# One bank for a whole output product, and a third accumulator for columns in place of a third for preparation

## The chip, the cores and the metric

The kernel runs on one core of one Trainium2 chip. The metric is the device time of one execution in microseconds (us), the median of several runs. A difference of less than about 1% can hardly be told from no change here.

## What is computed

One layer of an encoder is applied to two batches of 512 tokens by 1024 channels, with the same weights. Half of the mixed channels come from a bidirectional recurrence (RWKV-7), half from a two-dimensional neighbourhood attention:

```python
h = rms_norm(x, norm1_g)
proj = h @ w_in                                  # 1024 -> 3456 columns
rw_out = rwkv7_time_mix(shifted(proj[:, :1920])) # 512 channels, a scan in both directions
na_out = neighbourhood_attention(proj[:, 1920:]) # 512 channels, softmax over 8 x 16 neighbours
x = x + concatenate([rw_out, na_out], -1) @ w_out          # the output product
x = x + conv_ffn(x)                              # norm, w_up (1024 -> 5632), conv, gate, w_down
```

## The kernel before

Activations lie with channels on the 128 partitions and the 512 tokens along the row, so a weight column block is one PSUM bank of 128x512. Each such product is made of three matmuls per channel tile (high by high, low by high, high by low), to keep float32 accuracy.

`trunk` doesn't issue instructions. It records them, with a priority and with the tile that each reads and writes, and `Recorder.run` then makes one fixed order for each engine: at each step it takes, for the engine that comes free first, the ready instruction of the lowest priority number, by its own costs and latencies. A tile can only be placed once one of the buffers of its tag is free. `PBUFS` gives the number of PSUM banks of each tag: "mm" for columns of big products, "g" for the preparation of the recurrence and for the scores of the attention, and one bank each for "ch" (the chain of the scan), "y" and "x". They add up to eight. On the chip each engine works through its order as it stands.

The work goes in three stages.

- **Recurrence.** Eight groups (four channel tiles of batch 0, then of batch 1). `rwkv_prep`, `rwkv_products` (tiles `pg_G`) and `rwkv_turn` (`pg_V`, `pg_T`) prepare a group through the "g" banks; `rwkv_inverse` (`px_v`, `px_w`, `px_x`, and the short vector steps `tm`, `i_nr`) inverts 16 small triangles; `rwkv_chain` steps through eight chunks (`pch`, `py_y`). `proj` fills the rest of TensorE with columns of `w_in` (`pmm_in`), as work of low priority. The normalised input of one batch lies in 16 `H` tiles. They hold batch 0, then batch 1, and then batch 0 again (`norm1(0, False)`, tiles `po_x0nFalse`) for the columns that only the attention needs.
- **Attention.** Eight units, the four of batch 1 first (`ORDER = (1, 0)`). A unit's scores are `pg_sca`, its transposes `py_pta`, its sums `pch_oa` or `px_oa`, and its result goes through `py_ota` and `iW_ao` to the DRAM tile `mixd`.
- **Output product and feed-forward.** Columns of `w_out` in two halves: `w_out1` takes the four recurrence channel tiles of a batch, adds the input `x` and stores to the DRAM tiles `x1d` (product tiles `pmm_wp`); `w_out2` loads `x1d` again, multiplies the four attention channel tiles (`H_mb` or `AR_mb`, high and low) and adds. `norm2`, the `uf`, `up` and `dn` products follow.

```python
    w_out1(one)
    w_out1(two)
    w_out2(one)
    norm2(one)
```

Here `one` is batch 1 and `two` batch 0. `split_mix` loads four channel tiles of `mixd` through SyncE's queue, casts them (ScalarE) and makes the low parts (VectorE).

Of the kernel before, what the change touches and what calls it, by code (L numbers as in the profile page):

```python
# [20 lines left out]
P = 128  # L21
NB = 2
T = 512
# [8 lines left out]
STARTS = (0, 8, 24, 32)  # L32
GVB = 2
GAB = 1
PBUFS = {"mm": 2, "g": 3, "ch": 1, "y": 1, "x": 1}
BUFS = {
    "H": 16, "wr": 2, "wh": 3, "wl": 3, "po": 3, "gu": 4, "lora12": 2, "lora13": 2, "lora14": 2, 
    "AR": 2, "GV": GVB, "GA": GAB, "GR": 2, "UV": 2, "TT": 2, "bv": 2, "lw": 1, "ta": 1, "qd": 2, "rs": 2, "WC": 2, "Z": 2, "sw": 2,
# [6 lines left out]
ORDER = (1, 0)  # L45
# [14 lines left out]
MIXT = ("AR AR", "H " * 8)  # L60
# [6 lines left out]
X2T = (("UV", "UV"), ("GA", "BK"))  # L67
# [617 lines left out]
def trunk(ctx: ExitStack, tc: tile.TileContext, xT, win, wup, wout, wdn, lora_up, prm, cst, bias, out):  # L685
    nc = tc.nc
# [47 lines left out]
    def dram(name):  # L734
        return VTile([P, T], F32, real=dp.tile([P, T], F32, name=name))

    pd = [[dram(f"pd_{m}_{b}") for b in range(NB)] for m in range(NIN)]
    x1d = [[dram(f"x1d_{m}_{b}") for b in range(NB)] for m in range(8)]
    x2d = [[dram(f"x2d_{m}_{b}") for b in range(NB)] for m in range(8)]
    hd = [dram(f"hd_{m}") for m in range(8)]  # L740
    p1d = [dram(f"p1d_{m}") for m in range(NPRE)]
# [3 lines left out]
    nc = rec = Recorder(tc.nc, tc)  # L745
# [6 lines left out]
    def sb(tag, shape, name, dtype=F32):  # L752
        return sbp.tile(shape, dtype, tag=tag, name=f"{tag}_{name}", bufs=BUFS.get(tag, 1))

    def ps(tag, shape, name):
        return psp.tile(shape, F32, tag=tag, name=f"p{tag}_{name}", bufs=PBUFS[tag])

    first_w = list(FIRSTW)

    def load_w(src, n, name):  # L760
        pr = rec.prio
        rec.prio = first_w.pop(0) if first_w else min(pr, WPR)
        raw = sb("wr", [P, 4, P], name)
        nc.sync.dma_start(raw[:, :n], src)
        hi = sb("wh", [P, 4, P], name, F32R)
        nc.scalar.copy(hi[:, :n], raw[:, :n])
        lo = sb("wl", [P, 4, P], name, F32R)
        nc.gpsimd.tensor_tensor(lo[:, :n], raw[:, :n], hi[:, :n].bitcast(F32), ALU.subtract)
        rec.prio = pr
        return hi, lo  # L770

    def mm3(p, w, a, n, first, last):
        for k in range(n):
            ah, al = a(k)
            nc.tensor.matmul(p, w[0][:, k], ah, start=first and k == 0, stop=False)
            nc.tensor.matmul(p, w[0][:, k], al, start=False, stop=False)
            nc.tensor.matmul(p, w[1][:, k], ah, start=False, stop=last and k == n - 1)
# [53 lines left out]
    def wide(tags, name, dtype=F32):  # L831

        v = []
        for i, t in enumerate(tags.split()):
            n = 1 if t[0] == "H" or t[:4] == "lora" else 4
            x = sb(t, [P, n, T], f"{name}{i}", dtype)
            v += [x[:, j] for j in range(n)]
        return v
# [604 lines left out]
    rec.prio = 2 * FILL  # L1443
    banks = [t for t in PBUFS for _ in range(PBUFS[t])]
    nbank = [0]

    def bank(name):
        nbank[0] += 1
        return ps(banks[nbank[0] % 8], [P, T], name)

    x2, h2 = {}, {}

    one, two = ORDER

    def split_mix(b, k0, tags, name):

        v = wide(tags, f"{name}{b}", F32R)
        hi, lo = v[:4], v[4:8]
        for k in range(4):
            f = sb(("r", "k", "v", "i2")[k], [P, T], f"mx{b}{k0 + k}")  # L1460
            nc.sync.dma_start(f, mixd[k0 + k][b])
            nc.scalar.copy(hi[k], f)
            nc.vector.tensor_tensor(lo[k], f, hi[k].bitcast(F32), ALU.subtract)
        return hi, lo

    def gemm4(p, src, a, name):
        w = load_w(src, 4, name)
        mm3(p, w, lambda k: (a[0][k], a[1][k]), 4, True, True)

    def w_out1(b):  # L1470

        a = split_mix(b, 0, "GR GR", "ma")
        for n in range(8):
            p = ps("mm", [P, T], f"wp{n}{b}")
            gemm4(p, wout[n, :, :4], a, f"outa{n}{b}")
            x = sb(X1T[n % len(X1T)], [P, T], f"x1{b}{n}")
            nc.sync.dma_start(x, xT[b, :, n])
            nc.vector.tensor_add(x, x, p)
            nc.sync.dma_start(x1d[n][b], x)

    def w_out2(b):

        i = ORDER.index(b)
        a = split_mix(b, 4, MIXT[i], "mb")
        x2[b] = [sb(X2T[i][j], [P, 4, T], f"x2{b}{j}") for j in range(2)]
        for n in range(8):
            nc.sync.dma_start(x2[b][n // 4][:, n % 4], x1d[n][b])
        for n in range(8):
            p = ps("mm" if b == ORDER[0] else WOB[n % len(WOB)], [P, T], f"wo{n}{b}")
            gemm4(p, wout[n, :, 4:], a, f"outb{n}{b}")  # L1490
            xk = x2[b][n // 4][:, n % 4]
            nc.vector.tensor_add(xk, xk, p)
            nc.sync.dma_start(x2d[n][b], xk)

    def norm2(b):

        rs = sb("rs", [P, 4], f"f{b}")
        src = lambda k: x2[b][k // 4][:, k % 4]
        rms_scale(rms_sum(src, f"f{b}", lambda o, p, q: nc.vector.tensor_tensor(o, p, q, ALU.add), NTG[b == two]), rs, f"f{b}", NPS[b == two])
        if b == two:  # L1500
            v = wide(ACTB[1], f"g{b}", F32R)
            h2[b] = [None] * 4 + v[:4], [None] * 4 + v[4:]
        else:
            h2[b] = act_tiles(ACTB[0], f"g{b}")
        rms_split(src, row_scale(rs, f"f{b}", NPS[b == two]), lambda k: pv("n2g", k), *h2[b], f"f{b}", NPS[b == two], lambda k: nc.gpsimd.tensor_tensor if k % 4 in NPL else nc.vector.tensor_tensor, True)
        for k in range(8 if b == one else 0):
            nc.sync.dma_start(hd[k], src(k))
# [150 lines left out]
    G = {}  # L1658
    rec.prio = 1.5 * FILL
    mmb = lambda name: ps("mm", [P, T], name)  # L1660
    w_out1(one)
    w_out1(two)
    w_out2(one)
    norm2(one)
    halves_of("B11", one, 0)
    halves_of("B21", one, 1)
    w_out2(two)
    norm2(two)
    halves_of("B22", two, 1)
# [6 lines left out]
    for g, gn in enumerate(sizes):  # L1676
        for j in range(gn):
            up_pair(f0 + j, G, j)
        for n in range(8):
            w = load_w(wdn[n, :, f0 : f0 + gn], gn, f"dn{g}{n}")  # L1680
            for b in range(NB):
                p = bank(f"dn{g}{n}{b}")
# [3 lines left out]
                xk = sb(xl[nxl[0] % len(xl)], [P, T], f"xl{g}{n}{b}")  # L1686
# [64 lines left out]
```

## Time and profile before

| | |
|---|---|
| median of 3 runs | 1580.87 us (1577.47 to 1588.33) |
| the profiled execution | 1589.59 us, of which 1587.8 us are the span |
| TensorE (PE) busy | 1531.5 us, 96% of the span |
| VectorE (DVE) busy | 1195.3 us, 75% |
| ScalarE (ACT) busy | 800.1 us, 50% |
| GpSimd (POOL) busy | 286.4 us, 18% |
| HBM read, written | 152.05 MB, 57.67 MB |

The profiled execution is one execution; its time lies 0.55% above the median. PE is the engine that is nearly always busy. Matmuls overlap, so a busy PE is not PE at its best; how many matmuls start in a stretch, and how long it is idle, tells more.

### The profile page before, as it was taken

The numbers are of one execution on the slowest core, as the hardware profiler recorded it, in microseconds if no ns is written. First come the engines' busy times: TensorE is split into PE (matmuls) and PEld (weight loads), VectorE is DVE, ScalarE is ACT, GpSimd is POOL, SyncE is SP. The second block draws the span as 40 slices with busy tenths as digits, with TensorE's granted clock in tenths as the row PEclk, the third lists the DMA queues.
The fourth block names the chain that finished last, engine by engine and source line by source line (L and its number), as shares of the span: only waits on it lengthen the run. The fifth ranks groups of instructions, "written<-read, shape, count | busy, mean of one in ns | idle before, by whom it ended". The sixth has DMA issues, their size and how long they took to land.

```text
span 1587.8 us, 34480 instructions
## 1 busy us (share of the span) xinstructions
PE 1531.5 (96%) x13700; PEld 1210.2 (76%) x13700; DVE 1195.3 (75%) x2232; ACT 800.1 (50%) x1488; POOL 286.4 (18%) x284
## 2 busy tenths in 40 slices
PE   7997999999999999999998999999999999999998
PEld 5775777776777776788887877788788888888886
DVE  6878679877788675664685888959779578579666
ACT  5554565755655645577784454515335135234232
POOL 5223144321522312212230250000000000000000
PEclk8988999999999998999999999999999999999999
DMA  5522111222211225355777873383552631631535
GB/s 162 181 68 87 61 57 62 77 63 70 90 42 57 82 64 172 103 193 177 226 250 265 274 233 114 101 264 106 186 185 60 205 100 56 198 111 54 183 95 205
DMA packets 120401, 211.98 MB, mean 134 GB/s; under 512 B 13360, under 2 KB 22832, under 8 KB 120240
## 3 DMA queue, kind: packets, MB, share of 16 engines
q1 hardware_dynamic: 120096, 209.64, 40.6%
q8 instruction: 108, 1.77, 0.5%
q14 instruction: 53, 0.43, 0.1%
q10 hardware_dynamic: 144, 0.13, 0.0%
HBM read 152.05 MB, written 57.67 MB: 132 GB/s over the span
## 4 chain that ended last, share of the span: by engine, by line
PE 72%; DVE 7%; ACT 3%; DMA 2%; issue 2%; POOL 1%; SPq 0%; DVEq 0%; ACTq 0%; POOLq 0%
PE pmm_in L681 10%; PE pg_dn L681 6%; PE pmm_dn L681 4%; PE pch L681 2%; PE pmm_wp L681 2%; PE py_dn L681 2%; PE pch_dn L681 2%; PE px_dn L681 2%; PE pg_G L681 2%; PE py_y L681 1%; PE pmm_wo L681 1%; PE pg_T L681 1%; PE pg_sca L681 1%; PE px_x L681 1%; PE pg_wo L681 1%
## 5 line engine op out<-in xcount | busy, mean ns | idle before, releaser
L681 PE MATMUL pmm_in<-H_h,wh_in 128*128 128x512 f32 x848 | 311.3, 431 | 17.3 <-ACT H_h L681 6.2
L681 PEld LDWEIGHTS pmm_in<-H_h,wh_in 128*128 128x128 f32 x848 | 164.3, 199 | 57.8 <-issue 9.4
L681 PE MATMUL pmm_in<-H_h,wl_in 128*128 128x512 f32 x424 | 181.9, 429 | 5.2 <-DVE wl_in L681 2.8
L681 PEld LDWEIGHTS pmm_in<-H_h,wl_in 128*128 128x128 f32 x424 | 84.4, 199 | 23.2 <-DVE wl_in L681 4.0
L681 ACT CAST wh_in<-wr_in 128x512 fp32r<-128x512 f32 x108 | 66.4, 616 | 67.5 <-PE pmm_in L681 48.9
L681 DVE TENSOR_TENSOR wl_in<-wr_in,wh_in 128x512 fp32r<-128x512 f32 x82 | 62.5, 763 | 42.0 <-ACT wh_in L681 37.2
L681 ACT CAST wh_dn<-wr_dn 128x512 fp32r<-128x512 f32 (+1 forms) x48 | 27.8, 585 | 108.2 <-DMA wr_dn<-wdn_d 26.9
L681 PE MATMUL pg_G<-AR,BK 64*64 64x128 f32 x1024 | 69.2, 285 | 4.7 <-POOL BK L681 2.0
L681 POOL TENSOR_TENSOR wl_dn<-wr_dn,wh_dn 128x256 fp32r<-128x256 f32 x1 | 0.7, 738 | 374.3 <-ACT wh_dn L681 374.3
L681 PEld LDWEIGHTS pg_G<-AR,BK 64*64 64x64 f32 x1024 | 54.2, 137 | 16.7 <-issue 4.7
L681 POOL TENSOR_TENSOR sw<-S,WC 128x128 f32<-128x128 f32 x48 | 23.6, 492 | 180.1 <-DVE S L681 175.8
L681 ACT COPY UV<-pch 64x128 f32<-64x128 f32 x64 | 16.5, 258 | 68.8 <-DVE UV L681 42.9
L681 POOL TENSOR_TENSOR wl_in<-wr_in,wh_in 128x512 fp32r<-128x512 f32 x26 | 36.5, 1404 | 57.9 <-ACT wh_in L681 48.1
L681 DVE SCALAR_TENSOR_TENSOR po<-pmm_in,prm_s,po 128x511 f32<-128x511 f32 x58 | 43.2, 745 | 4.3 <-ACT po L681 3.6
L681 PE MATMUL pmm_wp<-GR_ma,wh_outa 128*128 128x512 f32 x128 | 44.2, 413 | 1.9 <-DVE Y_x L681 1.9
L681 ACT COPY i_na<-GA 32x512 f32<-32x512 f32 x32 | 35.0, 1094 | 19.5 <-DVE GA L681 19.1
L681 DVE SCALAR_TENSOR_TENSOR TT_ring<-pg_sca,rs_a,TT_ring 128x256 f32<-128x256 f32 x64 | 30.0, 478 | 16.7 <-PE pg_sca L681 9.4
L681 PE MATMUL pg_T<-cst_s,BK 64*64 64x64 f32 x1024 | 42.3, 221 | 0.0
L681 PEld LDWEIGHTS pg_T<-cst_s,BK 64*64 64x64 f32 x1024 | 36.7, 134 | 2.2 <-issue 1.2
L681 ACT ACTIVATE po_th<-ta_u 128x512 f32<-128x512 f32 x44 | 27.8, 632 | 19.6 <-DVE ta_u L681 13.4
L681 ACT ACTIVATE TT_ring<-TT_ring,mx_a 128x256 f32<-128x256 f32 x64 | 32.4, 507 | 5.1 <-DVE mx_a L681 4.6
L681 DVE TENSOR_TENSOR tm<-i_nr 128x15 f32<-128x15 f32 (+7 forms) x120 | 32.2, 269 | 2.5
(1903 smaller groups left out, 4568.6 us busy)
## 6 DMA issues: line engine op xcount, KB each, us to landing
wr_in<-win_d SPq DMA_DIRECT2D x108, 256.0 KB, 2.7
pd<-po SPq DMA_DIRECT2D x48, 256.0 KB, 2.1
GV_xl<-x2d SPq DMA_DIRECT2D x44, 256.0 KB, 4.0
wr_dn<-wdn_d SPq DMA_DIRECT2D x40, 256.0 KB, 2.7
x2d<-GV_xl SPq DMA_DIRECT2D x40, 256.0 KB, 3.1
i_up<-wup_d SPq DMA_DIRECT2D x33, 256.0 KB, 2.6
TT_ring<-bias_d SPq DMA_DIRECT2D x64, 128.0 KB, 2.7
up_xl<-x2d SPq DMA_DIRECT2D x22, 256.0 KB, 3.4
```

Of the source, the lines that this page charges most:

```text
L681: i.out = getattr(getattr(self.nc, i.eng), i.fn)(*[res(a) for a in i.args], **{n: res(a) for n, a in i.kw.items()})
```

## The change

`PBUFS` gives "mm" three banks and "g" two. For batch `one`, the two halves of the output product become one: a new `w_out` accumulates all eight channel tiles in one "mm" bank, loads `x` straight into the tile that `norm2` reads, and adds once. Batch `two` keeps its two halves.

```diff
-PBUFS = {"mm": 2, "g": 3, "ch": 1, "y": 1, "x": 1}
+PBUFS = {"mm": 3, "g": 2, "ch": 1, "y": 1, "x": 1}
...
-    x1d = [[dram(f"x1d_{m}_{b}") for b in range(NB)] for m in range(8)]
+    x1d = [dram(f"x1d_{m}") for m in range(8)]
...
+    def w_out(b):
+
+        a = split_mix(b, 0, "GR GR", "ma")
+        c = split_mix(b, 4, MIXT[ORDER.index(b)], "mb")
+        x2[b] = [sb(X2T[ORDER.index(b)][j], [P, 4, T], f"x2{b}{j}") for j in range(2)]
+        for n in range(8):
+            p = ps("mm", [P, T], f"wo{n}{b}")
+            w = load_w(wout[n, :, :4], 4, f"outa{n}{b}")
+            mm3(p, w, lambda k: (a[0][k], a[1][k]), 4, True, False)
+            w = load_w(wout[n, :, 4:], 4, f"outb{n}{b}")
+            mm3(p, w, lambda k: (c[0][k], c[1][k]), 4, False, True)
+            xk = x2[b][n // 4][:, n % 4]
+            nc.sync.dma_start(xk, xT[b, :, n])
             nc.vector.tensor_add(xk, xk, p)
             nc.sync.dma_start(x2d[n][b], xk)
...
-    w_out1(one)
     w_out1(two)
-    w_out2(one)
+    w_out(one)
     norm2(one)
```

Since the order is made anew, it differs nearly everywhere. Three places matter below.

The first is TensorE at the end of the attention. `py_ota30` is the last unit's last step; `mb02`, `mb03` are the high and `mb06`, `mb07` the low parts of the last two attention channel tiles of batch 0; `wp` and `wo` are the two halves of the output product, with column and batch behind them. Before:

```order
L681 MATMUL px_oa30_11006<-H_a305_10784,S_ring2_9172 128x64 x2
L681 MATMUL py_ota30_11131<-cst_s_62,H_a300_10074 128x128 x4
L681 MATMUL pmm_wp60_11137<-GR_ma00_10634,wh_outa60_11001 128x512
L681 MATMUL pmm_wp60_11137<-GR_ma01_10643,wh_outa60_11001 128x512
L681 MATMUL pmm_wp60_11137<-GR_ma00_10634,wl_outa60_11011 128x512
```

Now:

```order
L681 MATMUL px_oa30_11248<-H_a305_11054,S_ring2_9279 128x64 x2
L681 MATMUL py_ota30_11396<-cst_s_62,H_a300_9797 128x128 x4
L681 MATMUL pg_wo00_11315<-H_mb02_11412,wh_outb00_11100 128x512
L681 MATMUL pch_wo10_11257<-H_mb02_11412,wh_outb10_11153 128x512
L681 MATMUL pg_wo00_11315<-H_mb06_11414,wh_outb00_11100 128x512
L681 MATMUL pg_wo00_11315<-H_mb02_11412,wl_outb00_11114 128x512
L681 MATMUL pch_wo10_11257<-H_mb06_11414,wh_outb10_11153 128x512
L681 MATMUL pch_wo10_11257<-H_mb02_11412,wl_outb10_11161 128x512
L681 MATMUL pg_wo20_11351<-H_mb02_11412,wh_outb20_11223 128x512
L681 MATMUL pg_wo20_11351<-H_mb06_11414,wh_outb20_11223 128x512
L681 MATMUL pg_wo20_11351<-H_mb02_11412,wl_outb20_11239 128x512
L681 MATMUL pg_wo00_11315<-H_mb03_11433,wh_outb00_11100 128x512
```

Before, 24 matmuls of `wp` and then 96 of `wo` of batch 1 stood between the last unit and the first product that reads its batch's attention tiles; now all of those come earlier, and nine matmuls on `mb02` stand between `py_ota30` and the first that reads `mb03`.

The second place is VectorE where the `H` tiles take batch 0 again. Before:

```order
L681 SCALAR_TENSOR_TENSOR po_x0nFalse_8496<-po_x0nFalse_8496,prm_s,pmm_bca0False 128x512
L681 COPY UV_7953<-pch_8579 64x128
L681 TENSOR_TENSOR H_h_8592<-po_x0nFalse_8496,H_h_8576 128x512
L681 TENSOR_TENSOR S_8609<-pch_8579,WC_7275 128x128
L681 SCALAR_TENSOR_TENSOR po_x0nFalse_8541<-po_x0nFalse_8541,prm_s,pmm_bca0False 128x512
L681 TENSOR_TENSOR GV_8554<-GV_8554,pch_8579 128x128
L681 TENSOR_TENSOR H_h_8633<-po_x0nFalse_8541,H_h_8625 128x512
```

Now:

```order
L681 COPY UV_6962<-pch_7660 64x128
L681 TENSOR_TENSOR i_nr_7597<-i_nr_7597,tm_8064 128x11x5
L681 SCALAR_TENSOR_TENSOR po_x0nFalse_8138<-po_x0nFalse_8138,prm_s,pmm_bca0False 128x512
L681 TENSOR_TENSOR H_h_8234<-po_x0nFalse_8133,H_h_8214 128x512
L681 TENSOR_TENSOR tm_8064<-i_nr_7597 128x48
L681 TENSOR_TENSOR i_nr_7597<-i_nr_7597,tm_8064 128x12x4
L681 TENSOR_TENSOR H_h_8257<-po_x0nFalse_8138,H_h_8239 128x512
L681 TENSOR_TENSOR tm_8064<-i_nr_7597 128x39
L681 TENSOR_TENSOR wl_in_00_8269<-wr_in_00_7930,wh_in_00_8146 128x512
```

Before, the refill shared VectorE with the last chain (`UV`, `S`, `GV`), after the last inverse was done; now the refill comes one step of the recurrence earlier, among the steps of the last inverse (`tm`, `i_nr`).

The third place is TensorE in the preparation of group 3 (`pg_G3...`, beside the chain `pch_20` of group 2). Before:

```order
L681 MATMUL pg_G30011_3847<-AR_30_3438,BK_30_3447 64x128 x8
L681 MATMUL pg_G30100_3857<-AR_30_3438,BK_30_3447 64x128 x2
L681 MATMUL pg_G30101_3860<-AR_30_3438,BK_30_3447 64x128 x2
L681 MATMUL pg_G30100_3857<-AR_30_3438,BK_30_3447 64x128 x2
L681 MATMUL pg_G30101_3860<-AR_30_3438,BK_30_3447 64x128 x2
```

Now:

```order
L681 MATMUL pg_G30011_3886<-AR_30_3561,BK_30_3609 64x128 x8
L681 MATMUL pmm_in15_1_3788<-H_h112_1541,wh_in15_11_3767 128x512
L681 MATMUL pch_20_3743<-GV_200_3712,TT_20_2368 64x64 x4
L681 MATMUL pmm_in15_1_3788<-H_h14_1434,wl_in15_11_3818 128x512
L681 MATMUL pmm_in15_1_3788<-H_h15_1440,wh_in15_11_3767 128x512
L681 MATMUL pmm_in15_1_3788<-H_h113_1531,wh_in15_11_3767 128x512
L681 MATMUL pmm_in15_1_3788<-H_h15_1440,wl_in15_11_3818 128x512
L681 MATMUL pg_b30_3918<-ta_rk30_3908,bdr_65 128x512
L681 MATMUL pch_20_3743<-UV_20_3063,BT_20_3233 64x64 x4
L681 MATMUL pg_G30100_3929<-AR_30_3561,BK_30_3609 64x128 x8
```

Before, three product tiles followed each other in the three "g" banks; now a second tile of the pair is followed by columns and chain steps until a bank is read out.

## Rows read from the trace of the kernel before

**Rows 1.** The page: busy time, share of the span and instructions of each engine.

```profile
PE 1531.5 (96%) x13700; PEld 1210.2 (76%) x13700; DVE 1195.3 (75%) x2232; ACT 800.1 (50%) x1488; POOL 286.4 (18%) x284
```

**Rows 2.** Stretch, length; busy PE, PEld, DVE, ACT, POOL; granted clock, DMA share, GB/s.

```profile
150.00:600.00 450.00, 433.45 (x7946) 335.55 (x7934) 352.47 (x830) 263.85 (x490) 133.23 (x145) 0.99 0.22 69
600.00:650.00 50.00, 46.23 (x575) 31.43 (x573) 25.27 (x51) 23.15 (x44) 7.95 (x12) 0.91 0.38 124
650.00:850.00 200.00, 194.30 (x1261) 161.11 (x1256) 130.83 (x269) 150.56 (x360) 45.47 (x42) 0.98 0.64 205
850.00:900.00 50.00, 47.56 (x212) 38.18 (x211) 35.51 (x56) 22.30 (x38) 8.86 (x6) 1.00 0.77 256
1000.00:1200.00 200.00, 200.00 (x862) 161.22 (x861) 163.01 (x261) 76.05 (x120) 3.17 (x2) 1.00 0.50 162
```

**Rows 3.** Chain that ended last, end of the last attention unit: start, us, what.

```profile
847.60 0.66 PE py_ota L681 x4
848.26 2.76 PE pmm_wp L681 x11
...
853.32 4.06 DMA i_mx<-mixd
...
857.40 0.63 ACT H_mb L681
```

**Rows 4.** SP in order of time: the store of the last unit's result.

```profile
848.91 0.32 SPq L681 DMA_DIRECT2D mixd<-iW_aoa  x1
```

**Rows 5.** DMA issues of the page: count, KB each, median us to landing.

```profile
pd<-po SPq DMA_DIRECT2D x48, 256.0 KB, 2.1
```

**Rows 6.** Engines in ten-microsecond stretches, columns as in rows 2.

```profile
620.00:630.00 10.00, 6.97 (x44) 4.07 (x43) 7.55 (x14) 4.52 (x9) 2.06 (x2) 0.97 0.51 164
630.00:640.00 10.00, 10.00 (x44) 6.10 (x43) 5.10 (x10) 2.60 (x5) 0.41 (x1) 0.69 0.27 92
```

**Rows 7.** What PE waited for: total us, times, longest.

```profile
PE pmm_wp L681 <- DVE Y_x L681: 1.9, 2, 1.7
PE pmm_wo L681 <- DVE Y_x L681: 1.8, 1, 1.8
...
PE pmm_in L681 <- DVE po L681: 1.4, 1, 1.4
...
PE pmm_in L681 <- ACT po L681: 1.0, 1, 1.0
...
PE pg_G L681 <- DVE GR L681: 0.8, 2, 0.5
...
PE pmm_wo L681 <- DVE yo_x L681: 0.6, 1, 0.6
```

**Rows 8.** Groups of VectorE: busy us, mean ns of one | idle before, releaser.

```profile
L681 DVE TENSOR_TENSOR GA<-pg_G,cst 128x256 f32<-128x256 f32 x64 | 25.8, 418 | 10.4 <-PE pg_G L681 7.1 <-PE pch L681 2.7
...
L681 DVE STREAM_TRANSPOSE i_d<-i_rp 128x512 f32<-128x512 f32 x8 | 8.8, 1097 | 1.2 <-ACT i_rp L681 1.1
...
L681 DVE SCALAR_TENSOR_TENSOR po_x0nFalse<-po_x0nFalse,prm_s,pmm_bca0False 128x512 f32<-128x512 f32 x8 | 6.0, 746 | 3.2 <-DMA po_x0nFalse<-xT_d 3.1
L681 DVE TENSOR_TENSOR H_h<-po_x0nFalse,H_h 128x512 fp32r<-128x512 f32 x8 | 6.0, 755 | 2.0 <-ACT H_h L681 1.9
...
L681 DVE STREAM_TRANSPOSE i_l<-i_d 128x512 f32<-128x512 f32 x8 | 5.6, 706 | 0.1
...
L681 DVE TENSOR_TENSOR yo_x<-yo_x,pmm_wp 128x512 f32<-128x512 f32 x8 | 5.5, 683 | 0.1
...
L681 DVE TENSOR_TENSOR tm<-i_nr 128x15 f32<-128x15 f32 (+7 forms) x120 | 32.2, 269 | 2.5
```

**Rows 9.** PE in order of time where tile shapes change.

```profile
612.83 0.39 PE L681 MATMUL pmm_in<-H_h,wl_in 128*128 128x512 f32 x1
613.06 0.40 PE L681 MATMUL pmm_in<-H_h,wh_in 128*128 128x512 f32 x1
613.39 1.15 PE L681 MATMUL px_GV<-UV,GA 64*64 64x64 f32 x32
```

More of the change, by code (lines that the diff above doesn't have):

```diff
@@ L1478, in w_out1 @@
             nc.vector.tensor_add(x, x, p)
-            nc.sync.dma_start(x1d[n][b], x)
+            nc.sync.dma_start(x1d[n], x)
     def w_out2(b):
@@ L1486, in w_out2 @@
         for n in range(8):
-            nc.sync.dma_start(x2[b][n // 4][:, n % 4], x1d[n][b])
+            nc.sync.dma_start(x2[b][n // 4][:, n % 4], x1d[n])
         for n in range(8):
@@ L1491, in w_out2 @@
             xk = x2[b][n // 4][:, n % 4]
+            nc.vector.tensor_add(xk, xk, p)
+            nc.sync.dma_start(x2d[n][b], xk)
+    def w_out(b):
[10 more added lines that the diff above has]
+            nc.sync.dma_start(xk, xT[b, :, n])
             nc.vector.tensor_add(xk, xk, p)
```

## The prediction

> **What bounds the kernel now.** I read the page first. PE is busy for 96% of the span, VectorE for 75%, the others less [rows 1]. So the kernel is as long as PE's work plus what PE loses, and a change that leaves the matmuls as they are can only move the losses. This one leaves them: both versions have the same matmuls, 384 of them for the output product. Then I read PE by stretches [rows 2]. From 1000 to 1200 us, in the feed-forward, PE starts 862 matmuls in 200 us, 0.232 us each, at the full granted clock, without an idle moment; nothing is to be had there, and the change gives that part only other bank names. The losses lie earlier: 16.6 us idle between 150 and 600 us (the recurrence), 3.8 us between 600 and 650 with a clock of 0.91, 5.7 us in the attention (650 to 850) at 0.98, and 2.4 us between 850 and 900. A mean clock of 0.91 over 50 us is 4.5 us of work lost, since the granted clock has two levels, 2.4 and 1.2 GHz. The waits behind the idle time are short and many; those that a PSUM bank can be behind are in [rows 7]. VectorE, at 352 of 450 us in the recurrence [rows 2], reads the banks out, so it sets when a bank comes free.
>
> **The change part by part.** All terms stand against the profiled execution of 1589.59 us (span 1587.8, 1.8 around it).
>
> *The end of the attention.* Before, from the end of the last unit's transposes at 848.26 (847.60 plus 0.66) its result is copied, stored (issued at 848.91), loaded again (from 853.32, 4.06 until it lands) and cast (857.40 plus 0.63) [rows 3, 4]: 9.8 us until a matmul can read it. That cost nothing, as 120 other matmuls stood in between, 28 us at 0.232. In the new order nine stand there, 2.1 us. All the others have been moved ahead of it, into the attention. PE works in order, and what is queued behind the first matmul on `mb03` waits with it: 18 matmuls on this tile and 60 of the remaining columns. The feed-forward needs them all. So PE loses 9.8 less 2.1, **7.7 us**. Lower bound: two transfers at the 2.1 us of an unhurried store of the same size [rows 5] in place of 4.4 and 4.06, hence 3.5. Upper bound: stores of the normalised tiles (`hd`) and two loads of them now stand around this store and load in SP's queue, and three more transfers of 256 KB, at the 205 GB/s of the attention [rows 2], are 3.8 us, hence 11.5. I take the middle, as the measured chain already ran among such transfers.
>
> *The clock behind it.* Where PE was idle for 3.0 of 10 us, the next 10 us ran at a mean clock of 0.69, so 3.1 us of work were lost [rows 6]. A gap of 7.7 us should do as much: **+3.1 us**, bounds 0 and 5 (a stretch of 10 us wholly at the lower level).
>
> *The refill of `H`.* Before, it met the last chain and cost what [rows 6] shows: 3.0 idle, 0.3 and 3.1 by the clock, 6.4 us. Now the columns are further ahead and it meets the last inverse. From the chain's last copy (`UV`) to the inverse's second transpose, VectorE has 24 steps in the new order. From [rows 8]: four `H` parts at 0.755 (3.0), three scalings at 0.746 (2.2), a weight part taken at 0.755 (0.8), two transposes at 1.10 and 0.71 (1.8), nine short steps at 0.27 (2.4), and five of the normalisation of the output, three taken at 0.75 and two at 0.27 (2.8): 13.0 us. PE has 30 matmuls for it, 7.0 us. The gap is 6.0, with the clock 9.1, so **+2.7 us** more than before. Bounds: the three columns that can now stand open cover the hole (-6.4); or the loads of `x` come late as well, and none of the 30 matmuls fits in before the parts do (+9).
>
> *Two banks for the preparation.* A pair of `pg_G` tiles now fills both banks, and the next tile waits for three read-outs of 0.418 [rows 8]. Columns and chain steps fill that time in the new order, so the question is how often it is too short. I valued the matmuls between a bank's last use and the next tile in it by the trace's spacings: less than 1.5 us lie between at 69 of 269 places, before at 15 of 268. PE's stalls of this kind were 0.8 us [rows 7], 0.05 for each of the 15. The 54 more give **+3 us**. Bounds: nothing, and one whole read-out at each, 22.6 us. I take the low value since the row shows what such a place has cost.
>
> *Three banks for columns.* The waits of `pmm_in` for the read-out of a column, 1.4 and 1.0 [rows 7], should go: **-2.4 us** (bounds -2.4 and 0).
>
> *One bank for the whole product.* The waits of `pmm_wo` behind the additions of the first halves, 1.8 and 0.6 [rows 7], go: **-2.4 us**. The 1.9 of `pmm_wp` I leave, since batch 0 keeps its halves (bounds -4.3 and 0). Eight additions of 0.683 [rows 8] and 16 transfers of 256 KB go too. I cost them at nothing: VectorE is busy for 131 of 200 us there, the DMA engines for 0.64 [rows 2], and PE is the cover. Without it VectorE would give 5.5 us.
>
> *Tile shapes.* A large matmul before a smaller shape takes 0.33 in place of 0.23 [rows 9]. The new order changes shape 469 times in place of 487: **-1.8 us** (bounds -1.8 and 0).
>
> Sum: 7.7 + 3.1 + 2.7 + 3.0 - 2.4 - 2.4 - 1.8 = +9.9 us, or 0.62% of 1589.59. On the median of 1580.87 that is 1590.7, so **1591 us**.
>
> **Rivals.**
>
> *The two banks decide (slower).* Place: `pg_G`, `pg_V`, `pg_T` and the scores `pg_sca`. Price: one read-out of 0.418 at each of the 54 places, 22.6 in place of 3.0, so +29.5 us and 1610 us. It takes the result over 1% from 0.17 us a place. For it: VectorE does its work in a fixed order and other long steps stand between two read-outs. Against it: the stalls shown so far are 0.8 us. The Trainium skill speaks for it: its page "Perfetto Trace Analysis", section Matmuls under Optimizing Tensor Performance, wants independent groups of matmuls to rotate through different banks so that one is read out beside the next. By that rule preparation loses and columns gain; the columns' waits were only 2.4 us, so there is little to gain in the trade.
>
> *Mixing pays (faster).* The product's matmuls now stand among the attention's, and the columns run further ahead. If they fill the attention's 5.7 us idle and the 4 us that a clock of 0.98 over 200 us costs, half of the recurrence's 16.6 (8.3), and the hole at the refill (6.4), that is -24.4; with -6.6 for the waits and shapes, and the tail's +10.8, -20.2 us: 1561 us. For it: PE was waiting with more work at hand. Against it: the waits named in the recurrence are mostly for short vector steps, not for banks. The same page, section Optimization Strategy under Identifying Performance Opportunities, says that interleaving stages with different busiest engines can help. Here PE is the busiest in both, at 194 of 200 us in the attention [rows 2], which speaks against much of it.
>
> *The tail is covered after all (no change).* If on the chip the columns run late against the attention, PE still has products to do when the last unit is done, and the tail's 10.8 us fall away: -0.9 us, 1580 us. Against it: PE's order puts them ahead of the last unit's steps, so they would delay the unit with them.
>
> **How the numbers follow.** Forecast 0.40, two banks 0.22, tail covered 0.25, mixing 0.13. About a third of the forecast's own spread lies above 1597 (1%): the bounds of tail, clock and refill, all high, give +18 more. Slower by over 1% is then 0.22 and 0.13, 0.35; faster 0.13; the rest, 0.52, within 1%. A difference under about 1% can't be told from none by a measurement of this kernel. The range: the low bounds together give -11 us (1570), and I go to 1568 for the spread of the runs; above it takes in the two banks at 1610. It leaves out the mixing case and a little above: 1568 to 1612.
>
> **What would show it.** A gap of PE of 6 to 10 us behind the last `py_ota`, ended by the cast or the low part of `H_mb`, with the clock down behind it: the tail. PE idle for some 6 us while VectorE works on `po_x0nFalse` and `tm`: the refill. Waits of `pg_G`, `pg_T` and `pg_sca` for `GA`, `GR`, `BT` and `TT_ring` of 3 us in all: the banks; over 10 us, the first rival. No more waits of `pmm_wo` for `Y_x`. The feed-forward should take as long as before. I am wrong if the recurrence as a whole becomes shorter or longer by more than 10 us, which none of my terms but the banks would explain.

## The result, and the profile after

The changed kernel takes 1557.49 us (median of 4 runs; the kernel before 1579.74 beside it): a ratio of 0.9849, 95% interval 0.9811 to 0.9887. Timed again on another chip it took 1557.26 us, ratio 0.9822 (0.9807 to 0.9837). The forecast was 1591 us, the range 1568 to 1612: the sign was wrong and the range missed it. Of all executions reported below, three (one of the kernel with the late third bank, two of the changed kernel at 1450) ran at a granted clock of 0.55 to 0.65 and took 2057 to 2370 us, and no ratio or median here counts them.

The profiled execution of the changed kernel has a span of 1561.1 us, 26.7 less than that of before. The page's line of busy time, after:

```profile
PE 1518.8 (97%) x13700; PEld 1201.3 (77%) x13700; DVE 1190.2 (76%) x2231; ACT 798.6 (51%) x1488; POOL 282.8 (18%) x277
```

The matmuls are the same 13700 [rows 1], and PE is busy for 12.7 us less, idle for 14.0 less. Then the stretches of [rows 2], after, with the two that lie ahead of them (columns as there):

```profile
50.00:100.00 50.00, 48.87 (x311) 38.47 (x310) 44.44 (x72) 24.18 (x39) 18.89 (x16) 1.00 0.56 185
100.00:150.00 50.00, 48.20 (x683) 38.01 (x682) 46.03 (x86) 36.94 (x66) 24.69 (x18) 0.93 0.26 81
150.00:600.00 450.00, 435.81 (x7724) 335.50 (x7722) 356.01 (x846) 262.63 (x489) 127.10 (x143) 0.98 0.24 75
600.00:650.00 50.00, 49.55 (x642) 34.30 (x642) 20.05 (x49) 24.74 (x48) 6.14 (x11) 0.98 0.29 97
650.00:850.00 200.00, 196.81 (x1203) 163.27 (x1201) 140.08 (x276) 148.84 (x358) 44.25 (x39) 0.99 0.65 208
850.00:900.00 50.00, 44.90 (x185) 35.49 (x186) 37.16 (x55) 24.14 (x42) 14.55 (x10) 0.90 0.74 243
```

The same two early stretches before:

```profile
50.00:100.00 50.00, 48.32 (x266) 36.63 (x266) 38.43 (x62) 20.68 (x35) 13.69 (x13) 0.83 0.45 153
100.00:150.00 50.00, 41.90 (x408) 31.41 (x408) 44.77 (x84) 28.10 (x50) 19.13 (x17) 0.90 0.24 78
```

The largest single change stands between 50 and 150 us: 311 and 683 matmuls in place of 266 and 408, PE idle for 2.9 us in place of 9.8, and a clock of 1.00 and 0.93 in place of 0.83 and 0.90. The first chain's first matmul shows what came of it, before and then after:

```profile
171.75 0.27 PE L681 MATMUL pch<-GV,TT 64*64 64x64 f32 x2
```

```profile
153.48 0.27 PE L681 MATMUL pch<-GV,TT 64*64 64x64 f32 x2
```

18.3 us earlier, with 19 more column matmuls done (413 in place of 394, counted in the records). A second profile of the changed kernel has it at 155.0, and the last chain's last matmul (`pch`) starts at 644.6 us in place of 656.5. At 850 us the changed kernel has done 130 more big matmuls (counted in the records), 30 us at 0.232. It gives part of it back in the next stretch, where the tail is: 5.1 us idle, clock 0.90, against 2.4 and 1.00 [rows 2]. The feed-forward is as it was: from 1000 to 1200 us 863 matmuls in place of 862, and no idle time.

**Why PE stood still early.** PE's waits between 70 and 150 us before, in order of time (the last bracket is the idle time and what ended it):

```profile
75.09 0.50 PE L681 MATMUL pmm_in<-H_h,wl_in 128*128 128x512 f32 x1 [1.64 <-POOL wl_in L681]
122.66 0.70 PE L681 MATMUL pmm_in<-H_h,wh_in 128*128 128x512 f32 x2 [1.43 <-DVE po L681]
132.27 0.74 PE L681 MATMUL pmm_in<-H_h,wh_in 128*128 128x512 f32 x2 [1.51 <-ACT wh_in L681]
133.74 0.50 PE L681 MATMUL pmm_in<-H_h,wl_in 128*128 128x512 f32 x1 [0.73 <-POOL wl_in L681]
142.05 1.19 PE L681 MATMUL pmm_in<-H_h,wh_in 128*128 128x512 f32 x2 [4.31 <-DVE i_nr L681]
```

Only one of the five names the read-out of a column (`po`), and it is the 1.4 of [rows 7] that the prediction counted. The longest names `i_nr`, a step of the inverse that no column needs. VectorE in that time, before:

```profile
137.77 0.70 DVE L681 TENSOR_TENSOR pmm_in<-pmm_in,c_bcs 128x512 f32<-128x512 f32 x1 [1.49 <-PE pmm_in L681]
...
139.89 0.74 DVE L681 SCALAR_TENSOR_TENSOR po<-pmm_in,prm_s,po 128x511 f32<-128x511 f32 x1
140.55 0.70 DVE L681 TENSOR_TENSOR tm<-i_nr 128x15 f32<-128x15 f32 x1
141.17 0.74 DVE L681 SCALAR_TENSOR_TENSOR po<-pmm_in,prm_s,po 128x511 f32<-128x511 f32 x1
141.83 0.17 DVE L681 TENSOR_TENSOR i_nr<-i_nr,tm 128x15 f32<-128x15 f32 x1
...
142.75 0.69 DVE L681 TENSOR_TENSOR wl_in<-wr_in,wh_in 128x512 fp32r<-128x512 f32 x1
```

A column that PE has just finished is scaled at 137.77 and read out by two steps at 139.89 and 141.17, with steps of the inverse between them; PE goes on 0.14 us after the last one, and the trace names the short step next to it. By the order, the other "mm" bank is held at that time by a column whose second low weights VectorE makes only at 142.75. So, as I read it, two banks are both taken for 4.3 us, and a third would have held the next column. After, what is left of waits in that time:

```profile
78.40 0.50 PE L681 MATMUL pmm_in<-H_h,wl_in 128*128 128x512 f32 x1 [0.96 <-DVE wl_in L681]
98.77 1.09 PE L681 MATMUL pg_G<-AR,BK 64*64 64x128 f32 x16 [0.17 <-DVE GR L681]
128.67 0.50 PE L681 MATMUL pmm_in<-H_h,wl_in 128*128 128x512 f32 x1 [0.22 <-POOL wl_in L681]
137.78 1.97 PE L681 MATMUL pg_G<-AR,BK 64*64 64x128 f32 x16 [1.58 <-ACT ta L681]
```

The last of them is a wait for a bank too, now a "g" bank: `ta` is no input of `pg_G`, but what ScalarE reads out of `pg_a`, another tile of the "g" banks. The last part of `BK`, an input of this group, was done at 136.27 (135.58 plus 0.69):

```profile
135.58 0.69 DVE L681 TENSOR_TENSOR BK<-ta,iW 64x512 f32<-64x512 f32 x1
```

```profile
137.05 0.68 ACT L681 ACTIVATE ta<-pg_a,a0h 128x512 f32<-128x512 f32 x1
```

**The tail** is where it was forecast, and smaller than the 6 to 10 us that should have shown it. After, around the last unit's `py_ota` (PE, ScalarE, SyncE's queue, in order of time):

```profile
850.84 0.84 PE L681 MATMUL py_ota<-cst_s,H_a 128*128 128x128 f32 x4 [0.94 <-DVE H_a L681]
852.00 0.58 ACT L681 COPY iW_aoa<-py_ota 128x512 f32<-128x512 f32 x1
852.60 0.32 SPq L681 DMA_DIRECT2D mixd<-iW_aoa  x1
...
854.00 0.79 PE L681 MATMUL pg_wo<-H_mb,wh_outb 128*128 128x512 f32 x1 [2.33 <-ACT H_mb L681]
...
855.67 0.38 SPq L681 DMA_DIRECT2D i_mx<-mixd  x1
...
859.44 0.62 ACT L681 CAST H_mb<-i_mx 128x512 fp32r<-128x512 f32 x1 [5.49 <-DMA i_mx<-mixd]
...
860.11 0.50 PE L681 MATMUL pg_wo<-H_mb,wh_outb 128*128 128x512 f32 x1 [1.93 <-ACT H_mb L681]
```

The same store, load and cast as in [rows 3, 4], 8.4 us from the end of `py_ota` to the end of the cast, now with only a few matmuls beside them. PE waits twice, 4.3 us. Between the waits stand the nine matmuls on `mb02` that the prediction counted at 2.1 us; they took 4.2 (854.00 to the end of this one), since they ran 0.43 us apart and not 0.23. So part of what the clock lost filled the gap:

```profile
857.58 0.59 PE L681 MATMUL pg_wo<-H_mb,wl_outb 128*128 128x512 f32 x1
```

### The profile page after: what moved, and what is told of

It reads as the page before. It is cut to its first block, busy times and chain, and to the rows that moved or that the text cites. A ratio compares the mean times of both kernels' runs of the same rounds, so it can differ in the third digit from the quotient of the medians.

```text
span 1561.1 us, 34428 instructions
## 1 busy us (share of the span) xinstructions
PE 1518.8 (97%) x13700; PEld 1201.3 (77%) x13700; DVE 1190.2 (76%) x2231; ACT 798.6 (51%) x1488; POOL 282.8 (18%) x277
## 4 chain that ended last, share of the span: by engine, by line
PE 70%; DVE 8%; ACT 3%; issue 2%; DMA 0%; POOL 0%; SPq 0%; DVEq 0%; ACTq 0%; POOLq 0%
PE pmm_in L681 9%; PE pmm_dn L681 6%; PE pg_dn L681 4%; PE pmm_wo L681 2%; PE pch L681 2%; PE py_dn L681 2%; PE pch_dn L681 2%; PE px_dn L681 2%; PE pg_G L681 2%; PE pmm_wp L681 1%; PE py_y L681 1%; PE pg_sca L681 1%; PE py_pta L681 1%; PE px_oa L681 1%; PE pg_ssa L681 1%
## 5 line engine op out<-in xcount | busy, mean ns | idle before, releaser
L681 PE MATMUL pmm_in<-H_h,wh_in 128*128 128x512 f32 x848 | 302.2, 422 | 11.3 <-ACT H_h L681 7.7
L681 DVE TENSOR_TENSOR wl_in<-wr_in,wh_in 128x512 fp32r<-128x512 f32 x79 | 58.7, 744 | 35.1 <-ACT wh_in L681 28.5
L681 ACT COPY UV<-pch 64x128 f32<-64x128 f32 x64 | 16.6, 259 | 79.9 <-DVE UV L681 70.3
L681 POOL TENSOR_TENSOR wl_in<-wr_in,wh_in 128x512 fp32r<-128x512 f32 x29 | 42.3, 1459 | 56.6 <-ACT wh_in L681 33.6
L681 PE MATMUL pg_T<-cst_s,BK 64*64 64x64 f32 x1024 | 37.9, 222 | 0.2 <-ACT UV L681 0.2
L681 DVE COPY UV<-pch 64x128 f32<-64x128 f32 x64 | 18.8, 294 | 25.3 <-PE pch L681 18.7
L681 DVE TENSOR_TENSOR wl_dn<-wr_dn,wh_dn 128x512 fp32r<-128x512 f32 (+1 forms) x47 | 30.0, 645 | 4.9 <-ACT wh_dn L681 4.9
L681 PEld LDWEIGHTS pg_T<-cst_s,BK 64*64 64x64 f32 x1024 | 31.5, 134 | 2.0 <-issue 0.8
```

Of the source, the lines that this page charges most:

```text
L681: i.out = getattr(getattr(self.nc, i.eng), i.fn)(*[res(a) for a in i.args], **{n: res(a) for n, a in i.kw.items()})
```

## The experiments

The theories. T1: the third "mm" bank keeps PE fed at the start, while VectorE reads banks out late. T2: two "g" banks in place of three make a better order at the start. T3: it is the luck of one order; since the order is made anew, any edit moves the time. T4: the merged product.

**The two halves of the change.** The first kernel has only the banks, the second only the product:

```diff
-PBUFS = {"mm": 2, "g": 3, "ch": 1, "y": 1, "x": 1}
+PBUFS = {"mm": 3, "g": 2, "ch": 1, "y": 1, "x": 1}
```

```diff
...
-    w_out1(one)
     w_out1(two)
-    w_out2(one)
+    w_out(one)
...
```

> Three mm banks and two g banks, with the output product in its two old halves. Its order is that of the changed kernel up to the last chain. If the banks' numbers are the cause (theories 1 to 3), the first chain starts at 153 to 155 us as in the changed kernel, the clock in the first 150 us stays near 0.95, and the time is 1557 to 1566 us (ratio to before 0.985 to 0.991). If the merged product is the cause (theory 4), it is 1575 to 1585 us. My terms for the product's own part (waits of 2.4, tail gap of some 10 the other way) say that this kernel may even be a few us faster than the changed one.

> The merged output product with the old banks (two mm, three g). Its order is that of the kernel before up to the attention. If the banks are the cause, the first chain starts at 171 to 172 us as before, and the time is 1575 to 1590 us: the gap behind the attention (+8 to +11) against what the mixing with the attention gives back (-2 to -10). If the merged product is the cause (theory 4), it is 1560 us or less.

Banks only: 1567.86 us, ratio 0.9909 (0.9880 to 0.9939), first chain at 154.6 us. Product only: 1586.30 us, ratio 1.0010 (0.9986 to 1.0035), first chain at 172.9 us, and the early stretch is the old one:

```profile
100.00:150.00 50.00, 41.88 (x337) 31.63 (x334) 44.83 (x85) 28.46 (x49) 19.25 (x17) 0.90 0.27 84
```

T4 falls as the main cause: by itself the product is worth nothing. On top of the banks it goes with another 0.6 to 0.9% (0.9849 and 0.9822 against 0.9909). The gap behind the attention comes with the banks and not with the product, where both expectations put it: with the banks alone PE waits there for `H_mb` twice, 3.2 us; with the product alone not at all.

**Where the third bank pays.** Three kernels with two "mm" and two "g" banks and an eighth bank `z`: unused; for every third column of the first preparations; for every third column after these and every third product tile. Product in halves in all three.

```diff
-PBUFS = {"mm": 2, "g": 3, "ch": 1, "y": 1, "x": 1}
+PBUFS = {"mm": 2, "g": 2, "ch": 1, "y": 1, "x": 1, "z": 1}
...
+    ncol = [0]
+
+    def third():
+        ncol[0] += 1
+        return ("mm", "mm", "z")[ncol[0] % 3]
+
     def proj(m, b, bank="mm", raw=False):
+        if bank == "mm" and rec.group <= 2:
+            bank = third()
```

This is the second; the first has only the new `PBUFS`, and the third has `>= 3` and calls `third()` for `wp`, `uf` and the `wo` of batch `one` as well.

> Two mm banks, two g banks, and the eighth bank unused by recurrence and attention; the old halves of the product. Theory 1 (the third mm bank keeps PE fed at the start): first chain at 168 to 174 us, the clock near 0.84 from 50 to 150 us, 1578 to 1595 us. Theory 2 (with two g banks the work of the first group is done before that of the second): first chain at 152 to 158 us, 1560 to 1570 us. Theory 3 (only another order): anything between, with gaps at other places than in either.

> As the kernel with an idle eighth bank (two mm, two g), but that bank takes every third column of the first two preparations (columns filled in up to the second chain), and nothing later. If the third bank's worth lies at the start: first chain at 153 to 156 us, 3 us idle or less from 100 to 150 us, and 1570 to 1575 us in place of 1580. If it lies in the attention and the output product: first chain perhaps earlier, but within 3 us of 1580.

> The reverse: the eighth bank takes every third column from the third preparation on, and every third tile of the output product; the start has two mm banks. If the worth lies late: first chain at 158 us as with the idle bank, and 1566 to 1573 us, from more big matmuls done at 850 us (1580 to 1600 in place of 1531). If it lies at the start: within 3 us of 1580. If each has a share, this one and the reverse together gain some 12 us against 1580.

Idle: 1580.49 us, 0.9983 (0.9962 to 1.0003). Early: 1560.82 us, 0.9862 (0.9839 to 0.9885). Late: 1607.15 us, 1.0148 (1.0122 to 1.0175). The waits of PE in the kernel with the idle bank, 130 to 150 us:

```profile
132.87 0.73 PE L681 MATMUL pmm_in<-H_h,wh_in 128*128 128x512 f32 x2 [1.65 <-DVE po L681]
138.37 0.80 PE L681 MATMUL pmm_in<-H_h,wl_in 128*128 128x512 f32 x1 [2.17 <-POOL wl_in L681]
149.27 1.92 PE L681 MATMUL px_x<-i_d,i_x 32*32 32x32 f32 x64 [2.77 <-ACT i_x L681]
```

and its stretch from 100 to 150 us, then that of the kernel with the bank used early:

```profile
100.00:150.00 50.00, 43.06 (x632) 33.97 (x632) 46.84 (x82) 36.46 (x64) 27.41 (x20) 0.92 0.26 86
```

```profile
100.00:150.00 50.00, 48.07 (x733) 38.22 (x732) 48.39 (x90) 39.16 (x69) 25.08 (x20) 1.00 0.27 87
```

A third bank for five early columns takes 1.2% off the time of the idle one in this order, and brings it to 0.9862, where the whole change gives 0.9849 and 0.9822; that is some 10 us faster than I expected. PE is idle for 1.9 us from 100 to 150 us in place of 6.9, so T1 holds for the start. T2 is half right: with two "g" banks alone the first chain starts 13.5 us earlier (158.2), but the time doesn't follow. The third bank late is no help but 1.7% worse than idle: at 500 us 32 more big matmuls have been started and 524 fewer small ones (counted in the records), the last chain starts at 653.7 us in place of 610.1, and PE has little to put beside the end of the attention:

```profile
850.00:900.00 50.00, 40.98 (x225) 34.72 (x223) 33.45 (x70) 32.65 (x88) 9.75 (x6) 0.80 0.53 171
```

That fits columns that are good where PE would stand and bad where they stand in front of the recurrence; that the third bank and not just another order did it here is not shown.

**The wait at 75 us and the clock behind it.** Two neighbouring steps in GpSimd's order of the kernel before are exchanged, nothing else:

```diff
+        g = [k for k in order if ins[k].eng == "gpsimd"]
+        s, w = g[28], g[29]
+        p, q = order.index(s), order.index(w)
+        order[p : q + 1] = order[p + 1 : q + 1] + [s]
...
         self.emit(order)
```

> The kernel before with two neighbouring steps of GpSimd exchanged, and nothing else: the low part of the weights of column 6 (which PE waited for at 75.09 us, 1.64 us) now stands ahead of the sum of squares that it was queued behind. If that one wait is what brought the clock to 0.50 behind it, the wait is under 0.5 us, the clock from 70 to 100 us is 1.00 (8.2 us of work back), and PE has 270 to 280 columns' matmuls done at 100 us in place of 233. Is the lead kept, the first chain starts at 160 to 163 us and the time is 1572 to 1576 us. Is it lost again where two mm banks run out (120 to 150 us), the first chain starts at 168 us or later and the time is 1580 to 1585 us.

1586.14 us, 1.0016 (0.9995 to 1.0037). The wait went, from 1.64 to 0.19. From 80 to 90 us the clock is 1.00, where before it was at its lower level throughout (that row first, then the one with the exchange):

```profile
80.00:90.00 10.00, 10.00 (x54) 6.98 (x55) 5.62 (x12) 3.01 (x6) 4.35 (x4) 0.50 0.07 26
```

```profile
80.00:90.00 10.00, 10.00 (x100) 7.03 (x98) 9.96 (x19) 4.16 (x8) 5.64 (x6) 1.00 0.35 107
```

But only 248 column matmuls are done at 100 us (233 before, 270 to 280 expected), and the first chain starts 5.4 us earlier (166.3), between the two branches of the expectation. The wait for a bank is longer and ends earlier (L686 is the same line of `Recorder`, five further down):

```profile
136.02 1.19 PE L686 MATMUL pmm_in<-H_h,wh_in 128*128 128x512 f32 x2 [5.39 <-DVE i_nr L686]
```

The same column opens 6.0 us earlier than before (142.05), so in these two profiles most of the lead passes the full banks. In the medians there is none. The profiled execution of before lies above the median beside this run (1589.59 us, 1582.70), that of the exchange below its own (1582.75). So the clock's 8 us in the profile of before were not 8 us of the time; where the lead goes is not shown.

**The luck of the order.** One constant of the planner, in both kernels:

```diff
-DLAT, DMIN, DRATE = 1400, 500, 2.0
+DLAT, DMIN, DRATE = 1500, 500, 2.0
```

and so for 1350 and 1450.

> The kernel before, with banks and product as they were; one constant of the planner (its latency of a transfer) is 1500 in place of 1400, so that the order is made anew and differs from place 97 of PE on. Theory 3 (luck of the order): a change as large as that of the banks, 10 us or more either way, and the first chain shifted by 8 us or more. Theories 1 and 2: within 8 us of the kernel before, and the losses between 70 and 150 us stand where they stood.

> The changed kernel with the planner's latency of a transfer at 1500 in place of 1400, as was done to the kernel before (1605 us, 1.4% slower). If the banks help in any order: 1555 to 1585 us, 18 us or more below 1605. If the gain is luck of one order (theory 3): 1590 us or more.

> The kernel before in another order (the planner's latency of a transfer 1350 in place of 1400): 1570 to 1610 us, by the spread of the two orders so far (1584 and 1605). The start as with 1500: 8 to 12 us idle from 100 to 150 us.

> The changed kernel in the same second order. If the start's gain stays to the end in most orders: 10 to 25 us below the kernel before in that order. If the later order decides (as with 1500, where the pair stood 4 us apart): any difference from -25 to +20 us, with the start earlier all the same (first chain 8 us or more ahead, counted with its columns).

> The kernel before in a third new order (1450): 1570 to 1610 us.

> The changed kernel in that order: as for 1350. Over the four orders (1350, 1400, 1450, 1500) the mean difference says what the change is worth apart from the luck of one order: -15 us or more if the start's gain is kept, about -5 us if later steps take most of it.

| constant | before: us, ratio (interval) | changed: us, ratio (interval) | first chain, us | difference |
|---|---|---|---|---|
| 1350 | 1585.56, 1.0031 (1.0002 to 1.0060) | 1593.52, 1.0069 (1.0044 to 1.0094) | 166.7 to 159.9 | +0.4% |
| 1400 | 1585.37, 1 | 1557.26, 0.9822 (0.9807 to 0.9837) | 171.7 to 153.5 | -1.8% |
| 1450 | 1591.89, 1.0070 (1.0040 to 1.0100) | 1583.17, 1.0007 (0.9986 to 1.0029) | 173.7 to 163.7 | -0.6% |
| 1500 | 1604.58, 1.0142 (1.0114 to 1.0169) | 1600.51, 1.0117 (1.0094 to 1.0141) | 166.9 to 162.1 | -0.25% |

All ratios are to the kernel before. Each pair was timed side by side, but for that of 1500, timed on two chips. The mean of the four differences is -0.6%, 9 us, and they spread over 2.2%; four values so far apart do not tell this mean from nothing. The first chain is earlier in all four, but the time follows only in part: where the chain comes 18.3, 10.0 and 4.8 us earlier (1400, 1450, 1500) the time falls by 28, 9 and 4 us, and with 1350, where it comes 6.8 us earlier, the time rises by 8. There 27 fewer big matmuls are done by 175 us, and the third bank leaves the idle time from 100 to 150 us as long as it was, 7.4 us in place of 7.5:

```profile
100.00:150.00 50.00, 42.60 (x596) 33.74 (x596) 42.21 (x80) 34.78 (x60) 18.10 (x15) 0.83 0.22 70
```

With 1500 the changed kernel loses in the attention, which starts late (the last chain at 643.6 us, 616.8 with 1400):

```profile
650.00:850.00 200.00, 184.99 (x1182) 147.47 (x1182) 118.43 (x240) 126.45 (x292) 42.79 (x44) 0.91 0.51 165
```

against 195.84 and 0.97 in the kernel before at 1500, and 196.81 and 0.99 above. So T3 holds for most of the size of the result. The same test on the early third bank:

> Two mm, two g, the eighth bank idle, with the planner's latency at 1500: another order of the kernel that took 1580 us. By itself it only measures the luck of the order: 1570 to 1610 us. Expected at the start: the first chain at 158 to 162 us and 6 us idle or more from 100 to 150 us.

> The same order constant, with the eighth bank for every third column of the first two preparations. If the third bank at the start pays in any order, it is 10 to 20 us below the kernel with the idle bank, with 3 us idle or less from 100 to 150 us. If only the start gains but the later order decides the time, the start looks the same and the difference of the two times is under 8 us or of the other sign.

Idle 1598.97 us, 1.0075 (1.0054 to 1.0096); early 1603.91 us, 1.0111 (1.0083 to 1.0139). The idle kernel missed its expectation: its first chain starts at 171.8 us, later than the 166.9 of the kernel before at 1500, so what two "g" banks did for the start with 1400 (T2) they don't do in that order. With the early bank the start gains again, first chain at 162.4 us in place of 171.8, idle from 100 to 150 us 1.6 in place of 3.8. The time does not follow. From 220 to 240 us, where PE has few matmuls but chain steps, it is idle for 4.8 us at a low clock, with the idle bank for 1.0 (early first, then idle):

```profile
220.00:240.00 20.00, 15.20 (x125) 10.46 (x116) 18.16 (x31) 7.69 (x15) 10.01 (x11) 0.76 0.25 79
```

```profile
220.00:240.00 20.00, 19.00 (x306) 13.90 (x306) 17.78 (x30) 14.60 (x28) 11.40 (x11) 1.00 0.28 94
```

At 850 us the kernel with the early bank has started 92 more big matmuls, but its last chain ends 11 us later (the last `pch` at 670.0 us, 659.2), and from 850 to 900 us PE is idle for 9.2 us in place of 3.7.

**The tail, mended.** The changed kernel with two feed-forward columns of batch 1 ahead of the columns of batch 0's second half:

```diff
 def w_out2(b):
...
+        for m in range(2):
+            up_first(m)
         for n in range(8):
             p = ps("mm" if b == ORDER[0] else WOB[n % len(WOB)], [P, T], f"wo{n}{b}")
...
-    for m in range(NPRE):
+    for m in range(2, NPRE):
         up_first(m)
```

> The changed kernel, with the first two columns of the feed-forward that need batch 1 alone (48 matmuls, 11 us) set ahead of the second half of batch 0's output product. Its order is the changed kernel's up to the last attention unit. If the gap behind the last unit (4.3 us idle by two waits, and the clock behind it) is what it looks like, both waits on the last attention tiles go, the clock from 850 to 900 us is 0.97 or more, and the time is 1549 to 1555 us (5 to 8 us less; ratio 0.980 to 0.983). Rival: the 24 products of the half that filled PE between 837 and 850 us are now missing there, and the gap only moves to the front of the last unit: 1556 to 1562 us.

> The changed kernel itself, timed beside the one with the tail mended on the same chip: 0.982 to 0.988 of the kernel before.

> The kernel with the two feed-forward columns ahead of the second half of batch 0's product, once more. If the gap behind the attention costs what the profile says (4.3 us idle and up to 5 by the clock): 4 to 8 us below the changed kernel. If the gap had only moved: within 3 us of it.

First 1559.27 us, 0.9819 (0.9795 to 0.9842); then, on one chip with the changed kernel (1557.26, 0.9822), 1559.42 us, 0.9836 (0.9817 to 0.9856). No difference can be told. The stretches around the tail in the first of the two profiles:

```profile
800.00:850.00 50.00, 46.90 (x298) 38.33 (x297) 41.63 (x84) 39.65 (x100) 7.82 (x5) 1.00 0.62 202
850.00:900.00 50.00, 46.57 (x199) 36.56 (x198) 33.38 (x52) 22.61 (x38) 10.44 (x8) 0.97 0.72 234
```

The idle time behind the unit fell from 5.1 to 3.4 us, and that ahead of it rose from 1.4 (48.55 busy) to 3.1: the rival of the expectation. The clock from 850 us on is better by some 3 us of work (0.97 for 0.90); in the time that doesn't show, and why is open.

**Both good parts together**, the early third bank and the merged product:

> Two mm, two g, the eighth bank for every third column of the first two preparations (1561 us with the output product in halves), and the merged output product. Its order is that kernel's up to the recurrence's last steps. If merging pays wherever PE is ahead (as the step from 1568 with three mm banks to 1557 would say): 1550 to 1556 us. If the merged product is worth nothing by itself (as with the old banks, 1.001) : 1558 to 1563 us. If its gap behind the attention counts: 1565 us or more.

1564.54 us, 0.9845 (0.9823 to 0.9866), against 0.9862 in halves: the merged product adds nothing here either. So its 0.6 to 0.9% on top of three banks is a matter of that order, or small.

## Why the prediction was wrong

| term | forecast, us | what was found |
|---|---|---|
| gap behind the attention | +7.7 | two waits, 4.3; within the bounds (3.5 to 11.5); with the gap moved the time was the same (0.9819 and 0.9836 against 0.9822) |
| clock behind it | +3.1 | 0.90 over 44.90 busy us, 4.5; the bounds held |
| refill of `H` | +2.7 | about -0.6 |
| two "g" banks | +3.0 | waits for a read-out 2.7 in place of 0.8; in the time nothing told apart (0.9983 with the eighth bank idle) |
| three "mm" banks | -2.4 | about -12 in this order (0.9909 against 0.9983, three "mm" banks and an idle eighth); -19 with the third for early columns alone (0.9862) |
| one bank for the product | -2.4 | the waits for `Y_x` and `yo_x` went; alone 0 (1.0010); with three banks 0.6 to 0.9% |
| tile shapes | -1.8 | not measured apart; 469 changes in place of 487 in the records, but from a large matmul's shape to another 182 in place of 184 |

**The step that failed** is "Three banks for columns: -2.4 us (bounds -2.4 and 0)". Two mistakes are in it. I read PE's losses from 150 us on, so that the stretch from 50 to 150 us, with 9.8 us idle and clocks of 0.83 and 0.90, was in no term. And I took as the banks' cost only the waits that the profile puts down to a read-out. The 4.3 us put down to `i_nr` were, by VectorE's rows beside it, the bank's too. The bound of -2.4 was no bound: it held what had a name, not what a full bank could cause. In its place the runs show about -12 us for three "mm" banks in this order, and an early stretch with 2.9 us idle in place of 9.8. How the lead at the start becomes the time at the end stays open: it does not in every order. The prediction's own sign of being wrong, a recurrence shorter by more than 10 us, came: its last chain ends 11.9 us earlier.

Three of its numbers don't come out of its own working. The bounds of tail, clock and refill, all high, add 12 us (3.8, 1.9 and 6.3) and not 18. Behind the wait for `mb03` stood 9 matmuls on this tile (three columns of three) and not 18; the sum doesn't use them. And the price of a change of shape was read before a smaller shape, but taken for all 18 changes; by the records only two of them are of that kind, 0.2 us.

**Refill.** It now stands at 580 to 600 us, and PE's loss there is what it was in [rows 6]:

```profile
580.00:590.00 10.00, 9.18 (x158) 7.46 (x156) 7.89 (x18) 7.49 (x14) 5.92 (x5) 0.92 0.94 325
590.00:600.00 10.00, 8.54 (x122) 5.85 (x120) 4.94 (x8) 3.50 (x6) 3.56 (x4) 0.67 0.13 41
```

2.3 us idle and 3.5 by the clock, 5.8 in place of 6.4. The place was right, the 6.0 of gap were not. From `UV` (575.99) to the end of the second transpose (587.08) VectorE took 11.1 us in place of 13.0, and PE, which had small matmuls (`py_y`, `pg_T`, `pg_ssa`) beside the large ones, stood for 0.8 us of them.

**Two banks.** This term was about right as a wait. PE's waits for the read-out of a "g" bank, after (`ta` is read out of `pg_a`, `GR` out of `pg_G`; `pg_w` has no `ta` among its inputs):

```profile
PE pg_G L681 <- ACT ta L681: 1.6, 1, 1.6
PE pg_w L681 <- ACT ta L681: 0.9, 1, 0.9
PE pg_G L681 <- DVE GR L681: 0.2, 1, 0.2
```

2.7 us, where before there were the 0.8 of [rows 7]. The term looked for them at `GA`, `GR`, `BT` and `TT_ring`; they stand mostly at `ta`. In the other orders the same three waits are 11.4 us in place of 3.4 (1350), 3.3 in place of 2.7 (1450) and 5.2 in place of 2.2 (1500). That is 3.4 us more on the mean of four orders. With 1350, where the changed kernel is slower, it is 8.0:

```profile
PE pg_G L681 <- ACT ta L681: 6.6, 3, 3.2
PE pg_w L681 <- ACT ta L681: 1.7, 2, 1.5
PE pg_G L681 <- DVE GR L681: 3.1, 5, 1.7
```

A part of such a wait can be one for an input that came just before. The kernel with two "g" banks and an idle eighth shows none of it in the time: 0.9983. The rival of 1610 us falls for this order; in that of 1350 its mechanism is there, at a third of its price.

**The rival that came nearest** is "mixing pays", at 1561 us with a chance of 0.13; its number is right and its reasons mostly aren't. The attention gained 2.5 us idle and some 2 by the clock, not 9.7, the recurrence from 150 to 600 us 2.4 us idle (14.2 in place of 16.6), not 8.3, and the refill 0.6, not 6.4. What it said against itself, that waits in the recurrence are mostly for short vector steps and not for banks, has the same weakness as above: the step that is named need not be the one that is waited for. The page "Perfetto Trace Analysis" of the Trainium skill, section Matmuls under Optimizing Tensor Performance, wants groups of matmuls to rotate through banks so that a read-out overlaps the next group. I used it for the preparation's side of the trade; the runs bear it out on the columns' side in this order, 0.9862 against 0.9983 for a third bank at the start. Against it stand the third bank late, 1.0148, and the same early bank with 1500, 1.0111 against 1.0075.

**What I would still not have known.** Over four orders the change goes with -0.6% on the mean, with single orders from +0.4% to -1.8%. A forecast from the terms alone is a forecast of that mean at best. Still, the order of this kernel was there to be read, and the early stretch, counted whole, would have turned the sign of the sum: 9.8 us idle and some 12 by clocks of 0.83 and 0.90 are more than the +9.9 forecast. Counting it whole would have been luck in part, since the exchange at 75 us and the orders of 1350 and 1500 show that such a loss need not be time.

## What to carry to other kernels

Read the stretches from the first matmul on, and take the one with the worst mix of idle time and clock first, whatever the change is about. When a matmul that opens a bank waits for a short step of another engine, look up on that engine who read the bank last: the name at the wait can be that of a neighbour. Where a planner makes the order anew, time the change in several orders before believing its size. And try giving a resource to work of low priority only where it is needed: here, in one order, the third bank for early columns alone gave 0.9862, for the whole run 0.9909, and for the later columns 1.0148.

## What the runs showed of the hardware

The same program in the same order varies by 1% between executions, and with the granted clock: the kernel before took 1576.35 us at a mean clock of 0.989 and 1588.43 at 0.980, the changed one 1555.77 at 0.990 and 1562.90 at 0.983. The profile of before that I worked from was one of the longer ones, at 0.980 and 1589.59 us. Clock losses read from one profile are one draw: two profiles of the changed kernel (1562.90 and 1563.63 us) show 1.00 and 0.97 from 50 to 100 us, 0.93 and 0.97 from 100 to 150, and 0.90 and 0.86 from 850 to 900. Some come again: from 50 to 100 us the kernel before and the one with only the product, whose orders are the same there, both show 0.83, and taking the wait away brought the clock back there and not the time.

The last load of an attention tile takes 3.7 us from SyncE's issue to landing (855.67 to the cast at 859.44) against 2.1 for an unhurried store [rows 5]. It was issued 3.1 us after the store that it reads, with loads of `hd` put ahead of it in the queue.
